# Short gated convolution on token rows, with neighbours' terms added by DMAs within SBUF

## The chip, the cores and the metric

The kernel runs on one core of a Trainium2 chip. The engines of the core are named as the profile names them: PE multiplies matrices (PEld is its loading of weights), DVE, ACT and POOL work element by element, SP only issues DMAs. The time is that of one execution on the device, in microseconds (us). Before the change it is 1527.46 us, the median of three executions that lie between 1526.65 and 1527.49.

## The reference

The program is an encoder of two layers over 512 tokens of width 2048. In each layer the normalised input `h` is multiplied by one wide matrix, and the product's columns are shared out: latents for an attention, a query for an attention over 256 memory tokens, a gate, and the three operands of a short convolution, 512 channels each. What bears on the change is this part:

```python
def short_gated_conv(gb, gc, xin, w):
    u = gc * xin
    up = jnp.pad(u, ((0, 0), (1, 1), (0, 0)))
    conv = up[:, :-2] * w[0] + up[:, 1:-1] * w[1] + up[:, 2:] * w[2]
    return gb * conv

z = h @ w_in[l]
q_lat, kv_lat, k_pe, gb, gc, xin, q_mem, gate = split_cols(z)
c_out = short_gated_conv(gb, gc, xin, conv_w[l])
y = jnp.concatenate([a_out, c_out, m_out], axis=-1) * jax.nn.silu(gate)
x = x + rmsnorm(y @ w_o[l], post_norm_g[l])
```

Each output token of the convolution takes the gated input `u` of the token before it, of itself and of the token behind it, each with a weight per channel. Everything is float32.

## The kernel before

**Products.** Each float32 operand is split into a high part and a rest (`hi`, `lo`), and one product becomes three matmuls on PE: lines 296, 297 (the one that takes the weights' low part, `wl`) and 298. A block of the weight matrix is multiplied by a scheme of seven products, P1 to P7, where sums of weight quarters and sums of input quarters (A11, A12, A22, S1 to S4) are multiplied. One such *group* yields two outputs of 512 columns for all four token tiles of 128 rows.

**Units.** The weights of a group pass as units of 256 rows by two times 512 columns (512 KB). SP loads a unit into one of eight buffers `wr`, six units ahead. Where a pass needs a sum of quarters, DVE adds another block (L200), or an accumulating DMA issued by POOL adds it in the buffer (L142), as soon as the buffer's earlier content has been read. ACT casts the unit to its high part `wh` (L212), DVE subtracts to get the low part `wl` (L216), and PE uses both for twelve matmuls. There are three buffers each for `wh` and `wl`.

**Order of passes.** The first two groups of a layer hold the convolution's operands: group 0 gives `gc` and `xi`, group 1 gives `gb` and its gate `gg`. Their passes run as P1, P2 of group 0; P1, P2 of group 1; P5, P6, P3 with P7, P4 of group 0; the same of group 1. After them comes group 2. At the end of a pass, DVE adds PE's result to the output tile (L500, L530, L533). When both operands of a token tile are there, `fin_u` (L698) multiplies `gc` by `xi`, and in the next group `fin_g` applies Silu to the gate on ACT (L705) and multiplies `gb` by it (L707).

**The convolution** (`conv_turn`, L837 to L846) stands between the steps of group 2, four times per layer, once for every 128 channels. PE turns four 128x128 blocks of `gc` (L823, into a bank `tps`) so that channels lie on the partitions and tokens along the row. There the neighbour is one element off, and a weight is one value per partition: DVE multiplies by the middle weight (L841), adds the two shifted terms (L842, L843), and multiplies by the turned `gb` (L846). The result `y` is the left operand of the output projection.

**What sets the order.** PE, SP and POOL work in the order in which the program writes their instructions. DVE and ACT are ordered by a scheduler through most of the program, but each works through its own list in order. Small operations can be put off: `pr.defer(cost, fn)` puts one in a queue, and it is written once the steps of the program have gathered as much room as its cost:

```python
spare = min(spare + room, 2.5)
while self.queue and spare >= self.queue[0][0]:
    cost, put_off = self.queue.pop(0)
    spare -= cost
    put_off()
```

`pr.until(there)` writes the queue out until a condition holds.

Of the kernel before, what the change touches and what calls it, by code (L numbers as in the profile page):

```python
# [251 lines left out]
def encoder(tc, x, mem, positions, pre_norm_g, w_in, q_norm_g, w_uq, kv_norm_g, w_ukv, conv_w,  # L252
# [35 lines left out]
    def scrap(name, w=512, dt=F32):  # L288
        return piece.tile([P, 512], dt, tag="piece", name=nm(name))[:, :w]
# [25 lines left out]
    def setup():  # L315
        ident = scrap("ident", P)
        make_identity(nc, ident)
        identr = const.tile([P, P], F32R, name="identr")
        nc.vector.tensor_copy(identr, ident)
        mhalf = const.tile([P, 4], F32, name="mhalf")  # L320
        nc.gpsimd.memset(mhalf, -0.5)
        G.update(ident=identr.bitcast(F32), identr=identr, mhalf=mhalf, junk=const.tile([P, 512], mybir.dt.bfloat16, name="junk"))
        rows = scrap("rows", P)[:KT * 2 * depth + 18 * depth]
        n = KT * depth
        nc.scalar.dma_start(rows[:n], pre_norm_g.rearrange("l (k p) -> (l k) p", p=P))
        nc.scalar.dma_start(rows[n:2 * n], mem_norm_g.rearrange("l (k p) -> (l k) p", p=P))
        m = 2 * n + 12 * depth
        nc.scalar.dma_start(rows[2 * n:m], conv_w.rearrange("l k (c p) -> (l k c) p", p=P))
        nc.sync.dma_start(rows[m:m + 4 * depth], q_norm_g.rearrange("l (k p) -> (l k) p", p=P))
        nc.sync.dma_start(rows[m + 4 * depth:], kv_norm_g.rearrange("l (k p) -> (l k) p", p=P))  # L330
        G["rows"] = rows

    def turn_constants():
        rows = G["rows"]
        n = KT * depth
        o = 2 * n + 12 * depth
        m = o + 6 * depth
        ps = bank("cps")
        nc.tensor.transpose(ps[:, :m], rows, G["ident"][:m, :m])
        cols = const.tile([P, m], F32, name="cols")  # L340
        nc.vector.tensor_copy(cols, ps[:, :m])
        for l in range(depth):
            G[f"g1_{l}"] = cols[:, l * KT:(l + 1) * KT]
            G[f"gm_{l}"] = cols[:, n + l * KT:n + (l + 1) * KT]
            G[f"cw{l}"] = cols[:, 2 * n + 12 * l:2 * n + 12 * (l + 1)].rearrange("p (k c) -> p k c", k=3)
            G[f"cq{l}"] = cols[:, o + 4 * l:o + 4 * (l + 1)]
            G[f"ckv{l}"] = cols[:, o + 4 * depth + 2 * l:o + 4 * depth + 2 * (l + 1)]

# [326 lines left out]
    def projection(l):  # L675
        def block(cols, w):
            def f(h, j, c):
                r = h * 1024 + c * 256
                return w_in[l, r:r + 256, cols[j]:cols[j] + w].rearrange("(a p) c -> p a c", p=P)
            return f  # L680

        C = {}

        def own(*names):
            def f():
                for n in names:
                    C[n] = slab(n).rearrange("p (t c) -> p t c", t=NT)
            return f

        def slot_of(a, b):  # L690
            return lambda i, j, tt: C[(a, b)[j]][:, 2 * i + tt, :]

        def fin_u(i, j, tt):
            t = 2 * i + tt
            key = "u", t
            C[key] = C.get(key, 0) + 1
            if C[key] == 2:
                nc.vector.tensor_tensor(C["gc"][:, t, :], C["gc"][:, t, :], C["xi"][:, t, :], op=ALU.mult)  # L698

        def fin_g(i, j, tt):  # L700
            t = 2 * i + tt
            key = "g", t
            C[key] = C.get(key, 0) + 1
            if j == 1:
                nc.scalar.activation(C["gg"][:, t, :], C["gg"][:, t, :], AF.Silu)  # L705
            if C[key] == 2:
                nc.vector.tensor_tensor(C["gb"][:, t, :], C["gb"][:, t, :], C["gg"][:, t, :], op=ALU.mult)  # L707

        def own_lat():
            two = [slab("lat") for _ in range(2)]  # L710
            C["lat"] = [two[t // 2][:, (t % 2) * 1024:(t % 2) * 1024 + 832] for t in range(NT)]

        lat = lambda i, j, tt: C["lat"][2 * i + tt][:, j * 416:(j + 1) * 416]
        skip = lambda i, j, tt: None
        L = G["left"]
        gs = [
            group(L, (l, 0), 512, block((O_GC, O_XI), 512), slot_of("gc", "xi"), HEAD if l else FIRST, fin_u,
                  by_two=l == 0),
            group(L, (l, 1), 512, block((O_GB, O_G + 1024), 512), slot_of("gb", "gg"), HEAD, fin_g),
            group(L, (l, 2), 512, block((O_G + 1536, O_QM), 512), slot_of("gm", "qm"), STEADY, skip),  # L720
            group(L, (l, 3), 416, block((0, 416), 416), lat, STEADY, skip),
            group(L, (l, 4), 512, block((O_G, O_G + 512), 512), slot_of("ga0", "ga1"), STEADY, skip),
        ]
# [95 lines left out]
    def turn4(view, j, dst=None):  # L819

        ps = bank("tps")
        for t in range(NT):
            nc.tensor.transpose(ps[:, t * P:(t + 1) * P], view(t)[:, j * P:(j + 1) * P], G["ident"])  # L823
        return ps
# [11 lines left out]

    def conv_turn(l, c, C):  # L837
        def f():
            u = turn4(lambda t: C["gc"][:, t, :], c)
            y, w = y_slab(2)[:, c, :], G[f"cw{l}"]  # L840
            nc.vector.tensor_scalar_mul(y, u, w[:, 1, c:c + 1])  # L841
            nc.vector.scalar_tensor_tensor(y[:, 1:], u[:, :S - 1], w[:, 0, c:c + 1], y[:, 1:], op0=ALU.mult, op1=ALU.add)  # L842
            nc.vector.scalar_tensor_tensor(y[:, :S - 1], u[:, 1:], w[:, 2, c:c + 1], y[:, :S - 1],  # L843
                                           op0=ALU.mult, op1=ALU.add)
            g = turn4(lambda t: C["gb"][:, t, :], c)
            nc.vector.tensor_tensor(y, y, g, op=ALU.mult)  # L846
# [483 lines left out]
    G["src"], G["dst"] = x[0], None  # L1330
    for l in range(depth):
        G["left"] = L = Left(True)
        C, gs, owns = projection(l)

        def use(L=L):
            G["left"] = L
# [41 lines left out]
        if l == 0:  # L1378
            put(a[:1])
            add(first.close)  # L1380
            add(turn_half(1, 1))
            add(lambda: left_half(0, (1,)))
            add(lambda: left_half(1, (1,)))
            add(lambda: first_rows(2))
            add(lambda: first_factor(3))
            add(lambda: first_rows(3))
            put(a[1:], b[:1])
            add(turn[2])
            add(lambda: right_half(0))
            put(b[1:3])  # L1390
            add(turn[3])
            add(lambda: right_half(1))
            put(b[3:])
        else:
            put(a, b)
        add(owns[1])
        put(a1, b1)
        put(*gs[0][2:], *gs[1][2:])
# [100 lines left out]
```

## Time and profile before

| | |
|---|---|
| median of three executions | 1527.46 us |
| the profiled execution | 1528.12 us |
| its span | 1525.9 us |
| mean granted clock of PE | 0.995 |
| bytes moved by DMAs | 270.61 MB, mean 177 GB/s |
| matmuls on PE | 7613 |

The span runs from the first to the last recorded instruction of that execution. In the rows below, "x8" is a number of instructions, "128x512" is partitions by elements, and a releaser behind "<-" is what ended the idle time before an instruction. In a timeline the columns are start in us, duration in us, engine, line and operation, output and inputs. A row that stands for several instructions gives the time from the first one's start to the last one's end. A PE instruction's duration contains its way through the pipeline, so matmuls overlap, and it is their starts that tell the pace. In the rows of DMAs the last number is the median time from issue to landing.

### The profile page before, as it was taken

What the parts mean: (1) busy time and instruction counts of PE and PEld (TensorE: products, weight loads), DVE (VectorE), ACT (ScalarE), POOL (GpSimd) and SP (SyncE); (2) the same over time, 40 slices, a digit from 0 to 9 for tenths busy, and PEclk for the clock granted to TensorE, in tenths of its full rate; (3) what the DMA queues carried; (4) which work ended last, traced back from release to release, by engine and by line L of the source; (5) the groups of instructions that cost most, each with busy time, mean ns of one, the idle gap of its engine ahead of it and who ended that gap; (6) DMA issues with size and microseconds to landing.
All of it is one profiled execution on the core that took longest, in us unless ns stands there. A gap on an engine that the chain in (4) does not pass through costs nothing.

```text
span 1525.9 us, 20317 instructions
## 1 busy us (share of the span) xinstructions
PE 1490.4 (98%) x7613; PEld 1277.0 (84%) x7613; DVE 1157.1 (76%) x1502; ACT 868.8 (57%) x1339; POOL 186.6 (12%) x197
## 2 busy tenths in 40 slices
PE   8999999999999999999999999999999999999995
PEld 7788888987898888888788888888988888888884
DVE  5987887575887668887798877886676776689777
ACT  8643534454667768645498443534454686775543
POOL 0212020221000000011230112010221000002111
PEclk9999999999999999999999999999999999999998
DMA  8989695979464111399696899685978421037873
GB/s 310 221 215 234 175 197 153 204 195 255 131 214 158 42 34 64 106 201 285 191 349 222 224 228 235 187 185 155 201 198 201 152 70 41 29 108 151 279 167 124
DMA packets 144206, 270.61 MB, mean 177 GB/s; under 512 B 17160, under 2 KB 39788, under 8 KB 140780
## 3 DMA queue, kind: packets, MB, share of 16 engines
q1 hardware_dynamic: 108904, 191.15, 39.1%
q0 software_dynamic: 35072, 78.13, 26.5%
q8 instruction: 59, 0.97, 0.3%
q14 instruction: 39, 0.32, 0.1%
q10 hardware_dynamic: 132, 0.05, 0.0%
HBM read 254.61 MB, written 14.68 MB: 176 GB/s over the span
## 4 chain that ended last, share of the span: by engine, by line
PE 85%; DVE 6%; ACT 4%; issue 2%; DMA 1%; POOL 1%; DVEq 0%; POOLq 0%; SPq 0%; ACTq 0%
PE P L297 20%; PE P L298 20%; PE P L296 20%; PE ptp L1063 2%; DVE wl L216 2%; ACT wh L212 2%; PE tps L823 2%; PE o L297 1%; PE sc L296 1%; PE sc L297 1%; PE sc L298 1%; PE o L298 1%; PE o L296 1%; PE sc L1043 1%; PE sc L1044 1%
## 5 line engine op out<-in xcount | busy, mean ns | idle before, releaser
L212 ACT CAST wh<-wr 128x1024 fp32r<-128x1024 f32 (+1 forms) x404 | 415.8, 1033 | 473.5 <-PE P L298 278.4
L216 DVE TENSOR_TENSOR wl<-wr,wh 128x1024 fp32r<-128x1024 f32 (+1 forms) x404 | 480.9, 1194 | 222.7 <-ACT wh L212 219.7
L296 PE MATMUL P<-wh,S 128*128 128x512 f32 (+1 forms) x896 | 346.7, 387 | 0.0
L297 PE MATMUL P<-wl,S 128*128 128x512 f32 (+1 forms) x896 | 345.1, 385 | 1.7 <-DVE wl L216 1.7
L298 PE MATMUL P<-wh,S 128*128 128x512 f32 (+1 forms) x896 | 344.3, 384 | 0.7 <-DVE S L434 0.7
L297 PE MATMUL P<-wl,A 128*128 128x512 f32 (+1 forms) x656 | 252.4, 385 | 6.3 <-DVE wl L216 6.3
L296 PE MATMUL P<-wh,A 128*128 128x512 f32 (+1 forms) x656 | 253.3, 386 | 0.9 <-ACT wh L212 0.9
L298 PE MATMUL P<-wh,A 128*128 128x512 f32 (+1 forms) x656 | 251.6, 384 | 0.5 <-DVE A L434 0.5
L297 PEld LDWEIGHTS P<-wl,S 128*128 128x128 f32 x896 | 168.7, 188 | 32.9 <-DVE wl L216 3.8
L298 PEld LDWEIGHTS P<-wh,S 128*128 128x128 f32 x896 | 168.5, 188 | 31.9 <-DVE S L434 1.1
L296 PEld LDWEIGHTS P<-wh,S 128*128 128x128 f32 x896 | 168.6, 188 | 29.7
L142 POOL DMA_DIRECT2D wr<-in_w_in_dram x84 | 101.6, 1210 | 554.1 <-DVE wl L216 400.4
L297 PEld LDWEIGHTS P<-wl,A 128*128 128x128 f32 x656 | 123.2, 188 | 29.7 <-DVE wl L216 8.4
L296 PEld LDWEIGHTS P<-wh,A 128*128 128x128 f32 x656 | 123.1, 188 | 23.8 <-ACT wh L212 2.1
L298 PEld LDWEIGHTS P<-wh,A 128*128 128x128 f32 x656 | 123.2, 188 | 23.4 <-DVE A L434 1.2
L200 DVE TENSOR_TENSOR wr<-wr,wr 128x1024 f32<-128x1024 f32 (+1 forms) x100 | 118.6, 1190 | 8.5 <-DMA wr<-in_w_in_dram 6.4
L1049 ACT ACTIVATE P<-sc,nm 128x512 f32<-128x512 f32 (+1 forms) x96 | 59.9, 625 | 36.7 <-DVE nm L1046 36.0
L1046 DVE TENSOR_REDUCE nm<-sc 128x1 f32<-128x512 f32 (+1 forms) x96 | 56.9, 595 | 12.3 <-PE sc L1044 6.8
L1052 ACT ACTIVATE P<-P,rec 128x512 f32<-128x512 f32 (+1 forms) x96 | 61.5, 658 | 5.9 <-DVE rec L1051 5.9
L142 POOL DMA_DIRECT2D wr<-in_w_o_dram x32 | 38.7, 1210 | 197.5 <-DVE wl L216 123.9
L302 DVE TENSOR_TENSOR PT<-ptp,PT 128x512 fp32r<-128x512 f32 (+1 forms) x96 | 56.1, 593 | 8.8 <-ACT PT L301 8.6
L226 ACT ACTIVATE wh<-wr,cols 128x512 fp32r<-128x512 f32 x64 | 43.9, 718 | 21.7 <-PE mk L297 7.7
(270 smaller groups left out, 2240.0 us busy)
## 6 DMA issues: line engine op xcount, KB each, us to landing
wr<-in_w_in_dram SPq DMA_DIRECT2D x172, 512.0 KB, 4.4
wr<-in_w_o_dram SPq DMA_DIRECT2D x72, 512.0 KB, 4.5
wr<-in_w_in_dram POOLq DMA_DIRECT2D x68, 512.0 KB, 7.2
wr<-in_w_in_dram SPq DMA_DIRECT2D x40, 416.0 KB, 3.8
wr<-in_w_o_dram POOLq DMA_DIRECT2D x32, 512.0 KB, 7.3
wr<-in_w_mk_dram SPq DMA_DIRECT2D x16, 512.0 KB, 5.3
wr<-in_w_mv_dram SPq DMA_DIRECT2D x16, 512.0 KB, 6.1
wr<-in_w_in_dram POOLq DMA_DIRECT2D x16, 416.0 KB, 5.9
```

The costliest lines, as they stand in the source:

```text
L142: engine.dma_start(dst, src, **kw)
L200: nc.vector.tensor_tensor(src, src, tiles[c], op=ALU.add)
L212: nc.scalar.copy(hi[:, :n], src)
L216: nc.vector.tensor_tensor(lo[:, :n], src, hi[:, :n].bitcast(F32), op=ALU.subtract)
L226: nc.scalar.activation(hi[:, h], src[:, h], AF.Copy, scale=g)
L296: nc.tensor.matmul(ps, ah, bh, start=first, stop=False, **kw)
L297: nc.tensor.matmul(ps, ah, bl, start=False, stop=False, **kw)
L298: nc.tensor.matmul(ps, al, bh, start=False, stop=last, **kw)
L302: nc.vector.tensor_tensor(lo, src, hi.bitcast(F32), op=ALU.subtract)
L1046: nc.vector.tensor_reduce(nmax, ps, axis=AX.X, op=ALU.max, negate=True)
L1049: nc.scalar.activation(pt, ps, AF.Exp, bias=nmax, accum_out=tot)
L1052: nc.scalar.activation(pt, pt, AF.Copy, scale=rec)
```

## The change

The convolution is computed with tokens on the partitions.

- The weights of the three taps come as rows, each sent to all 128 partitions by SP (`conv_rows`, 256 KB each). The columns of weights that the setup turned are gone.
- After L698 (now L696) three multiplies per token tile are put off with a cost of 0.7: `xi` becomes `u` times the middle weight, a new slab `zc` becomes `u` times the first, and `gc` becomes `u` times the last (L703).
- Behind the last of these twelve taps POOL issues four accumulating DMAs within SBUF. They add `zc` one partition down (L708) and `gc` one partition up (L709), 127 partitions of 2048 elements each, and then the rows that pass from one token tile to the next (L710, L711). L709 waits for L708 and L710 for L709, since they write the same slab.
- `fin_g` puts off one more multiply per token tile, `gb` by the finished `xi` (`weigh`, L728). The first of them waits for all four DMAs.
- `conv_turn` turns only `gb` (four transposes in place of eight), and ACT copies the bank to `y`.

```diff
@@ fin_u
             if C[key] == 2:
                 nc.vector.tensor_tensor(C["gc"][:, t, :], C["gc"][:, t, :], C["xi"][:, t, :], op=ALU.mult)
+                for k, name in ((1, "xi"), (0, "zc"), (2, "gc")):
+                    pr.defer(0.7, lambda k=k, name=name: taps(k, name, t))
+
+        def taps(k, name, t):
+            if name == "zc" and t == 0:
+                own("zc")()
+            nc.vector.tensor_tensor(C[name][:, t, :], C["gc"][:, t, :], C["w", k], op=ALU.mult)
+            if (k, t) != (2, NT - 1):
+                return
+            y, a, b = (C[n].rearrange("p t c -> p (t c)") for n in ("xi", "zc", "gc"))
+            n = (NT - 1) * 512
+            nc.gpsimd.dma_start(y[1:], a[:P - 1], accum_op=ALU.add)
+            nc.gpsimd.dma_start(y[:P - 1], b[1:], accum_op=ALU.add)
+            nc.gpsimd.dma_start(y[:1, 512:], a[P - 1:, :n], accum_op=ALU.add)
+            nc.gpsimd.dma_start(y[P - 1:, :n], b[:1, 512:], accum_op=ALU.add)
+
+        def conv_rows():
+            for k in range(3):
+                C["w", k] = scrap(f"cw{k}")
+                nc.sync.dma_start(C["w", k], conv_w[l, k].partition_broadcast(P))
@@ fin_g
                 nc.vector.tensor_tensor(C["gb"][:, t, :], C["gb"][:, t, :], C["gg"][:, t, :], op=ALU.mult)
+
+                def weigh():
+                    nc.vector.tensor_tensor(C["gb"][:, t, :], C["gb"][:, t, :], C["xi"][:, t, :], op=ALU.mult)
+                    C["conv"] = C.get("conv", 0) + 1
+                pr.defer(0.7, weigh)
@@ conv_turn
-            u = turn4(lambda t: C["gc"][:, t, :], c)
-            y, w = y_slab(2)[:, c, :], G[f"cw{l}"]
-            nc.vector.tensor_scalar_mul(y, u, w[:, 1, c:c + 1])
-            nc.vector.scalar_tensor_tensor(y[:, 1:], u[:, :S - 1], w[:, 0, c:c + 1], y[:, 1:], op0=ALU.mult, op1=ALU.add)
-            nc.vector.scalar_tensor_tensor(y[:, :S - 1], u[:, 1:], w[:, 2, c:c + 1], y[:, :S - 1],
-                                           op0=ALU.mult, op1=ALU.add)
-            g = turn4(lambda t: C["gb"][:, t, :], c)
-            nc.vector.tensor_tensor(y, y, g, op=ALU.mult)
+            pr.until(lambda: C.get("conv") == NT)
+            nc.scalar.copy(y_slab(2)[:, c, :], turn4(lambda t: C["gb"][:, t, :], c))
@@ main
             add(lambda: right_half(1))
+            add(conv_rows)
             put(b[3:])
         else:
-            put(a, b)
+            put(a)
+            add(conv_rows)
+            put(b)
```

The change moves lines (L696 in the new kernel is L698 before, L498 is L500, L531 is L533, L725 is L707) and the running numbers of tiles, but the number right behind `wl` and `wh` still counts the units. Three places in the lists of the engines matter below.

The first is DVE in layer 0 where group 1's P5 begins. `wl36` to `wl39` are the four units of that P5; L500 (L498) adds P4 of group 0, which shares the banks of its P6, and completes `gc` of the last two token tiles. Before:

```order
L216 TENSOR_TENSOR wl36_1074<-wr28_951,wh36_1073 128x1024
L200 TENSOR_TENSOR wr34_1016<-wr34_1016,wr35_1018 128x1024
L216 TENSOR_TENSOR wl37_1092<-wr30_971,wh37_1091 128x1024
L500 TENSOR_TENSOR gc_31_272<-gc_31_272,P6_70_798 128x512
L500 TENSOR_TENSOR gc_31_272<-gc_31_272,P6_71_799 128x512
L698 TENSOR_TENSOR gc_31_272<-gc_31_272,xi_32_273 128x512 x2
L216 TENSOR_TENSOR wl38_1116<-wr32_992,wh38_1115 128x1024
L216 TENSOR_TENSOR wl39_1138<-wr34_1016,wh39_1137 128x1024
```

With the change:

```order
L703 TENSOR_TENSOR zc_82_1022<-gc_31_271,cw0_57_519 128x512
L216 TENSOR_TENSOR wl36_1085<-wr28_956,wh36_1084 128x1024
L703 TENSOR_TENSOR gc_31_271<-gc_31_271,cw2_59_523 128x512
L200 TENSOR_TENSOR wr30_976<-wr30_976,wr31_978 128x1024
L498 TENSOR_TENSOR gc_31_271<-gc_31_271,P6_73_803 128x512
L498 TENSOR_TENSOR gc_31_271<-gc_31_271,P6_74_804 128x512
L216 TENSOR_TENSOR wl37_1104<-wr30_976,wh37_1103 128x1024
L696 TENSOR_TENSOR gc_31_271<-gc_31_271,xi_32_272 128x512 x2
L703 TENSOR_TENSOR xi_32_272<-gc_31_271,cw1_58_521 128x512
L200 TENSOR_TENSOR wr32_997<-wr32_997,wr33_999 128x1024
L200 TENSOR_TENSOR wr34_1025<-wr34_1025,wr35_1027 128x1024
L703 TENSOR_TENSOR zc_82_1022<-gc_31_271,cw0_57_519 128x512
```

The next row is `wl38`. Four more taps stand above this piece, two behind the first pair of L696, one behind `wl33` and one ahead of the first row, so that eight of the twelve taps stand between that pair and `wl38`; two sums (L200, of `wr32` and `wr34`) have moved from ahead of `wl37` to behind it. The other four taps stand between `wl40` and `wl43`.

The second place is DVE at the end of group 1 in layer 0, where the last pass (P4) takes its units from `wl52` on and L725 gates `gb`. Before:

```order
L216 TENSOR_TENSOR wl53_1407<-wr30_971,wh53_1406 128x1024
L707 TENSOR_TENSOR gb_57_540<-gb_57_540,gg_58_541 128x512 x2
L533 SCALAR_TENSOR_TENSOR gg_58_541<-P7_85_1296,gg_58_541 128x512
L500 TENSOR_TENSOR gb_57_540<-gb_57_540,P7_85_1296 128x512
L533 SCALAR_TENSOR_TENSOR gg_58_541<-P7_86_1297,gg_58_541 128x512
L500 TENSOR_TENSOR gb_57_540<-gb_57_540,P7_86_1297 128x512
L216 TENSOR_TENSOR wl54_1431<-wr32_992,wh54_1430 128x1024
```

With the change:

```order
L216 TENSOR_TENSOR wl53_1431<-wr30_976,wh53_1430 128x1024
L725 TENSOR_TENSOR gb_60_545<-gb_60_545,gg_61_546 128x512 x2
L728 TENSOR_TENSOR gb_60_545<-gb_60_545,xi_32_272 128x512 x2
L531 SCALAR_TENSOR_TENSOR gg_61_546<-P7_89_1318,gg_61_546 128x512
L498 TENSOR_TENSOR gb_60_545<-gb_60_545,P7_89_1318 128x512
L531 SCALAR_TENSOR_TENSOR gg_61_546<-P7_90_1319,gg_61_546 128x512
L498 TENSOR_TENSOR gb_60_545<-gb_60_545,P7_90_1319 128x512
L216 TENSOR_TENSOR wl54_1455<-wr32_997,wh54_1454 128x1024
```

Two of the new multiplies stand ahead of the four P7 rows and of `wl54`, and the first of them is the instruction that waits for the DMAs. In layer 1 the first pair of P7 rows stands ahead of L725, and the unit behind is `wl292`.

The third place is POOL in layer 0, with the change; the rows of L142 are the last two accumulates for P4 of group 1 and then the first for group 2:

```order
L142 DMA wr32_997<-in_w_in_dram 128x2x512
L142 DMA wr34_1025<-in_w_in_dram 128x2x512
L708 DMA xi_32_272<-zc_82_1022 127x2048
L709 DMA xi_32_272<-gc_31_271 127x2048
L710 DMA xi_32_272<-zc_82_1022 1x16x96
L711 DMA xi_32_272<-gc_31_271 1x16x96
L142 DMA wr44_1365<-in_w_in_dram 128x2x512
```

Before, the accumulate of `wr44` stands directly behind that of `wr34`; now four DMAs stand between them.

More of the change, by code (lines that the diff above doesn't have):

```diff
@@ L322, in setup @@
         G.update(ident=identr.bitcast(F32), identr=identr, mhalf=mhalf, junk=const.tile([P, 512], mybir.dt.bfloat16, name="junk"))
-        rows = scrap("rows", P)[:KT * 2 * depth + 18 * depth]
+        rows = scrap("rows", P)[:KT * 2 * depth + 6 * depth]
         n = KT * depth
@@ L326, in setup @@
         nc.scalar.dma_start(rows[n:2 * n], mem_norm_g.rearrange("l (k p) -> (l k) p", p=P))
-        m = 2 * n + 12 * depth
-        nc.scalar.dma_start(rows[2 * n:m], conv_w.rearrange("l k (c p) -> (l k c) p", p=P))
+        m = 2 * n
         nc.sync.dma_start(rows[m:m + 4 * depth], q_norm_g.rearrange("l (k p) -> (l k) p", p=P))
@@ L335, in turn_constants @@
         n = KT * depth
-        o = 2 * n + 12 * depth
+        o = 2 * n
         m = o + 6 * depth
@@ L344, in turn_constants @@
             G[f"gm_{l}"] = cols[:, n + l * KT:n + (l + 1) * KT]
-            G[f"cw{l}"] = cols[:, 2 * n + 12 * l:2 * n + 12 * (l + 1)].rearrange("p (k c) -> p k c", k=3)
             G[f"cq{l}"] = cols[:, o + 4 * l:o + 4 * (l + 1)]
@@ L724, in projection @@
         owns = [own("gc", "xi"), own("gb", "gg"), own("gm", "qm"), own_lat, own("ga0", "ga1")]
-        return C, gs, owns
+        return C, gs, owns, conv_rows
     def mem_load():
@@ L1332, in encoder @@
         G["left"] = L = Left(True)
-        C, gs, owns = projection(l)
+        C, gs, owns, conv_rows = projection(l)
         def use(L=L):
```

## The prediction, made before the changed kernel was run

> **What bounds the kernel now.** I read the busy shares first, then the chain of waits, then what PE waited for.
>
> ```profile
> span 1525.9 us, 20317 instructions
> PE 1490.4 (98%) x7613; PEld 1277.0 (84%) x7613; DVE 1157.1 (76%) x1502; ACT 868.8 (57%) x1339; POOL 186.6 (12%) x197
> PE 85%; DVE 6%; ACT 4%; issue 2%; DMA 1%; POOL 1%; DVEq 0%; POOLq 0%; SPq 0%; ACTq 0%
> PE P L297 <- DVE wl L216: 8.0, 10, 2.1
> ```
>
> PE is busy 98% of the span and carries 85% of the chain; its longest list of waits is 8.0 us in ten pieces, all for a low part `wl` that DVE makes. So the kernel is PE-bound, and the change can act in two ways only: it takes work from PE, or it makes PE wait where it does not wait now. DVE at 76% looks as if it had room, but that is a mean. I therefore read the stretches where the change puts DVE work, as busy times by engine (PE, weight loads, DVE, ACT, POOL), then granted clock, DMA share and GB/s:
>
> ```profile
> 109.91:127.39 17.48, 17.48 (x79) 14.46 (x78) 17.48 (x22) 7.00 (x7) 2.42 (x2) 1.00 0.87 271
> 127.39:137.50 10.11, 10.11 (x46) 8.40 (x45) 4.88 (x6) 3.54 (x4) 4.51 (x4) 1.00 1.11 199
> 908.53:926.02 17.49, 17.49 (x79) 14.49 (x78) 17.49 (x23) 6.80 (x7) 2.40 (x2) 1.00 0.85 266
> 194.00:214.00 20.00, 20.00 (x104) 16.84 (x103) 16.36 (x20) 7.70 (x9) 3.64 (x3) 1.00 0.84 184
> ```
>
> Where the gated input is finished and the taps will land (109.91 to 127.39 in layer 0, 908.53 to 926.02 in layer 1) DVE has no idle time at all, and PE none either. Just behind (127.39 to 137.50) DVE is busy 4.88 of 10.11 us. Where the convolution is done now (194 to 214) PE never waits, so DVE work removed there buys nothing.
>
> **What leaves PE.** Eight turns of four 128x128 transposes go (four of `gc` per layer). The stream of PE around one pair of turns:
>
> ```profile
> 194.25 0.39 PE L298 MATMUL P<-wh,A 128*128 128x512 f32 x1
> 194.48 0.60 PE L823 MATMUL tps<-identr,gc 128*128 128x128 f32 x4
> 194.91 0.60 PE L823 MATMUL tps<-identr,gb 128*128 128x128 f32 x4
> 195.27 0.48 PE L296 MATMUL P<-wh,S 128*128 128x512 f32 x1
> ```
>
> Products start 0.23 us apart (194.25 to 194.48), so eight transposes add 195.27 − 194.25 − 0.23 = 0.79, or 0.40 a turn. Eight turns: **−3.2 us**.
>
> **What leaves DVE and comes to ACT.** Per turn go L841, L842, L843 (of L842's form) and L846: 0.75 + 0.74 + 0.74 + 0.69 = 2.9 us of DVE. One ACT copy of the same form as L834 (597 ns) comes.
>
> ```profile
> L841 DVE TENSOR_SCALAR y<-tps,cols 128x512 f32<-128x512 f32 x8 | 6.0, 749 | 5.1 <-PE tps L823 5.1
> L842 DVE SCALAR_TENSOR_TENSOR y<-tps,cols,y 128x511 f32<-128x511 f32 x8 | 6.0, 744 | 0.0
> L846 DVE TENSOR_TENSOR y<-y,tps 128x512 f32<-128x512 f32 x8 | 5.5, 689 | 0.8
> L698 DVE TENSOR_TENSOR gc<-gc,xi 128x512 f32<-128x512 f32 x8 | 5.1, 680 | 0.0
> L834 ACT ACTIVATE y<-tps x24: 586/597/641, 376.0 to 1214.9; 128x512 f32<-128x512 f32 x24
> ```
>
> PE waits for none of the four, and ACT is busy 7.70 of 20 us there, so the copies hide: 0 and 0. Without that cover eight copies would cost 4.8 us.
>
> **Twelve taps per layer.** Each is a 128x512 multiply within SBUF like L698 (680 ns). Back to back such operations start 0.60 apart, as two do here, and the low part behind the second L698 pair ends at 127.39:
>
> ```profile
> 109.91 1.28 DVE L530 TENSOR_TENSOR xi<-P,xi 128x512 f32<-128x512 f32 x2
> 111.10 1.28 DVE L698 TENSOR_TENSOR gc<-gc,xi 128x512 f32<-128x512 f32 x2
> 122.64 1.22 DVE L216 TENSOR_TENSOR wl<-wr,wh 128x1024 fp32r<-128x1024 f32 x1
> 126.18 1.21 DVE L216 TENSOR_TENSOR wl<-wr,wh 128x1024 fp32r<-128x1024 f32 x1
> 132.45 1.23 DVE L216 TENSOR_TENSOR wl<-wr,wh 128x1024 fp32r<-128x1024 f32 x1 [3.42 <-ACT wh L212]
> 123.98 0.39 PE L297 MATMUL P<-wl,S 128*128 128x512 f32 x1
> 129.42 0.39 PE L297 MATMUL P<-wl,S 128*128 128x512 f32 x1
> 924.80 2.35 DVE L216 TENSOR_TENSOR wl<-wr,wh 128x1024 fp32r<-128x1024 f32 x2
> 926.97 0.39 PE L297 MATMUL P<-wl,S 128*128 128x512 f32 x1
> ```
>
> The order shows eight taps ahead of wl38, the third unit of P5 in the second group. PE first uses the first unit at 123.98; a unit is 12 products of 0.227, 2.72 us, so the third is due at 123.98 + 5.44 = 129.42. Since DVE has no gap before, eight taps (8 × 0.60 = 4.8) push its end from 127.39 to 132.2: PE waits **2.8 us**. The first two units stay in time by the same count: ahead of wl37 stand six taps and the two P6 evacuations more (3.6 + 1.2) but two sums L200 less (of wl37's size, 1.14 apart), so 2.5 more, from an end of 123.86 (the row at 122.64) to 126.4, with 126.70 as the due time. The last four taps (2.4) fall into gaps like the one of 3.42: 0. In layer 1 the order is the same at wl276, which ends at 926.02 (half of the pair at 924.80) and is due at 926.97: 4.8 − 0.95 = **3.85 us**. The price is not in doubt, since the form is L698's.
>
> **The weighting.** Two of the four new L728 stand ahead of wl54 (layer 0) and wl292 (layer 1), each 0.60.
>
> ```profile
> 167.82 1.29 DVE L707 TENSOR_TENSOR gb<-gb,gg 128x512 f32<-128x512 f32 x2 [0.72 <-ACT gg L705]
> 171.43 2.35 DVE L216 TENSOR_TENSOR wl<-wr,wh 128x1024 fp32r<-128x1024 f32 x2
> 172.94 0.39 PE L297 MATMUL P<-wl,A 128*128 128x512 f32 x1
> 968.28 2.35 DVE L216 TENSOR_TENSOR wl<-wr,wh 128x1024 fp32r<-128x1024 f32 x2
> 970.60 0.39 PE L297 MATMUL P<-wl,A 128*128 128x512 f32 x1
> ```
>
> wl54 ends at about 172.64 and is due at 172.94, a slack of 0.30; wl292 at 969.50, due 970.60, a slack of 1.10. Two L728 take 1.2: **0.9** and **0.1 us**.
>
> **The four accumulating DMAs.** The first L728 waits for all four, and behind it on DVE, which works in order, stand four P7 evacuations and wl54, so a late DMA goes to PE in full. Budget: POOL is free after its last P4 accumulate.
>
> ```profile
> 141.72 1.22 POOL L142 DMA_DIRECT2D wr<-in_w_in_dram  x1 [1.33 <-DVE wl L216]
> wr<-in_w_in_dram POOLq DMA_DIRECT2D x68, 512.0 KB, 7.2
> mTd<-mH POOLq DMA_DIRECT2D x2, 1024.0 KB, 5.3
> mH<-mTd POOLq DMA_DIRECT2D x2, 1024.0 KB, 9.6
> mL<-mTd POOLq DMA_DIRECT2D x2, 1024.0 KB, 12.7
> g<-in_post_norm_g_dram POOLq DMA_DIRECT2D x8, 256.0 KB, 6.4
> rows<-in_pre_norm_g_dram ACTq DMA_DIRECT2D x1, 16.0 KB, 1.7
> ```
>
> That is 142.9, plus PE's 2.8 and the four late taps' 2.4: 148.1. The first L728 is ready at 169.0 + 2.8 = 171.8, so 23.7 us are there. The chain is two transfers of 1016 KB one after the other, three further issues of 1.2 each (POOL's row) and a 6 KB landing. No row shows an accumulate within SBUF. Bounds: 2 × 5.3 + 3.6 + 1.7 = 15.9 and 2 × 12.7 + 3.6 + 6.4 = 35.4 (the landings of 16 KB and, far off, 256 KB), late by 0 or 11.7. I take 9.6 for each (512 KB accumulates take 7.2, and the first queues behind one) and 2.4 for the landing, near the 16 KB row: 19.2 + 3.6 + 2.4 = 25.2, **1.5 us late**, twice, since layer 1 has 0.5 us more at most between the same two points (926.97 to 965.88 against 129.42 to 167.82, where I take L707's start at 965.88).
>
> ```profile
> 965.88 1.29 DVE L707 TENSOR_TENSOR gb<-gb,gg 128x512 f32<-128x512 f32 x2
> ```
>
> [...]
>
> **Loads.** Three 256 KB broadcast loads per layer stand ahead of weight loads on SP. By the 6.4 of the broadcast `g` they hold the queue 19 us at worst, against six units of 2.72 that are loaded ahead, 16.3: 0 to 2.9 a layer, taken as 0, since transfers overlap. The 2 MB that the DMAs move share engines with weight loads that have units in hand too: 0.
>
> **Sum:** 2.8 + 3.85 + 0.9 + 0.1 + 3.0 − 3.2 = +7.45, on the profiled execution's 1528.12: 1535.6. That execution is 0.66 above the median of 1527.46, so **1535 us**.
>
> **The rivals.**
> (A, the forecast) Stalls at the third P5 unit and at the DMAs: with the DMAs late by 0 and 11.7 per layer, +4.5 to +27.9, or 1532 to 1555; its own likely range is 1531 to 1546, since the upper end needs the worst row for both transfers in both layers. Chance 0.74.
> (B) The stalls come, but a later PE waits less elsewhere. For it: 8.0 us of waits on `wl` exist, some of them after layer 0. Against: PE waits for nothing between 109.91 and 137.50, so nothing close by gives back. With the DMAs in time and half of the 8.0 recovered: +0.5, 1528. Chance 0.13.
> (C, the other side) The taps fit, the DMAs are in time, and only PE's relief remains: 1527.46 − 3.2 = 1524.3. Decided at 109.91 to 127.39: eight taps would have to take under 2.03 us, 0.25 each. Against: 17.48 of 17.48 busy. Chance 0.05.
> (D) The 127-row transfers are not spread over the DMA engines. Price by the software queue's row:
>
> ```profile
> q0 software_dynamic: 35072, 78.13, 26.5%
> ```
>
> 78.13 MB took 0.265 × 16 × 1525.9 = 6470 engine-us, 12.1 KB per us and engine. One engine alone would need 86 us for 1.04 MB, two in series 172; less the budget of 24, DVE stands about 148 us per layer, and PE with it: 1527.5 + 4.5 + 296 = 1828. [...] Against: all the queue's rows here have 128 partitions and show nothing of odd counts. Chance 0.08. [...]
>
> **How the numbers follow.** The time is A's, 1535. About 0.2% (3.05 us) can be told from no change, so slower means above 1530.5: nearly all of A with D and none of C, 0.80; B with A's lowest edge, 0.14; C, 0.06. The range leaves out C and D and holds A with most of B: 1529 to 1548.
>
> **What would show it.** Right: PE waiting on L297 for `wl` by 2 to 4 us near 130 and 928, and for one or two near 175 and 972; L728's idle time released by L709 to L711; no `tps<-gc`. If L728 shows no idle, the DMA term was too large (1532); if both transfers take 13 us, too small (1541 and more). Wrong at the root: no new wait of PE at the third P5 unit (then DVE's stretch was not the bound), or a gap of 100 us and more at L728 (D).

## The result: 1556 us, slower by more than was forecast

| | median, us | lowest to highest | executions |
|---|---|---|---|
| before | 1527.49 | 1526.65 to 1528.25 | 5 |
| with the change | 1556.13 | 1552.09 to 1558.71 | 5 |

The ratio is 1.0185, with a 95% interval of 1.0174 to 1.0196: 28.6 us slower. The forecast was 1535, 7.5 slower, with a range of 1529 to 1548. The direction was right, the size was not.

The page of the changed kernel, busy times first, then the chain that ended last; behind it the view of PE's waits (us in total, times, longest):

```profile
span 1554.9 us, 20277 instructions
PE 1498.1 (96%) x7581; PEld 1278.9 (82%) x7581; DVE 1154.5 (74%) x1502; ACT 873.3 (56%) x1347; POOL 192.8 (12%) x205
PE 67%; DVE 10%; DMA 9%; issue 8%; ACT 5%; POOL 1%; SPq 0%; DVEq 0%; POOLq 0%; ACTq 0%
```

```profile
PE P L297 <- DVE wl L216: 18.8, 19, 2.6
PE P L296 <- ACT wh L212: 10.9, 6, 5.3
```

PE's share of the chain fell from 85% to 67%, and DMAs went from 1% to 9%. The waits for `wl` rose from 8.0 to 18.8 us, as the prediction said they would. But there is a second list it had not expected: 10.9 us of waits for the high part `wh`, one of them 5.3 us long. And PE is busy 7.7 us longer although it has 32 instructions fewer, so some of its products ran slower.

The two traces hold the same products in the same order, so each can be set beside its twin. The growing difference of their start times splits the loss of the two profiled executions (in us):

| where (us in the changed kernel) | layer 0 | layer 1 |
|---|---|---|
| stalls at taps (119 to 134, 933 to 948) | 3.5 | 3.3 |
| stall at a unit loaded behind L708 (166, 979) | 6.8 | 4.6 |
| stall at `wl54` and `wl292`, behind L728 (189, 1000) | 2.8 | 1.7 |
| stall at the first turn of the convolution (215, 1024) | 1.8 | 0.9 |
| turns that are gone | −1.7 | −1.7 |
| products at a lower clock, and rest | 3.7 | 3.4 |
| sum | 16.9 | 12.2 |

The stall at the first turn is not one for the turn: PE waits there for a low part behind a sum (L200) that waited 5.74 us for a load. The largest row is the second. Its timeline on PE and ACT, and the windows behind it (busy time of PE, weight loads, DVE, ACT, POOL; then granted clock, DMA share, GB/s):

```profile
160.39 0.39 PE L298 MATMUL P<-wh,S 128*128 128x512 f32 x1
166.04 0.80 PE L296 MATMUL P<-wh,S 128*128 128x512 f32 x1 [5.26 <-ACT wh L212]
164.94 1.05 ACT L212 CAST wh<-wr 128x1024 fp32r<-128x1024 f32 x1 [9.91 <-DMA wr<-in_w_in_dram]
```

```profile
160.50:166.00 5.50, 0.28 (x2) 0.00 (x0) 0.00 (x0) 1.05 (x1) 0.84 (x1) 0.96 1.01 312
166.00:172.20 6.20, 5.70 (x13) 4.14 (x14) 4.92 (x5) 1.99 (x2) 0.00 (x0) 0.50 1.07 165
```

PE waits for a cast, and the cast waits for the load of its weights. No engine of the core was late; a transfer was. After the stall the clock granted to PE is 0.50 for some six us, and a product takes 0.43 us from start to start instead of 0.23.

The transfers of that stretch, by the view of DMA issues: first five weight loads of the kernel before, issued from 143 to 155 us, then those of the changed kernel issued from 147 to 158, with the DMAs of POOL beside them.

```profile
q1 hardware_dynamic: 1063, 2.05, 52.5%
q0 software_dynamic: 499, 0.95, 43.4%
wr<-in_w_in_dram SPq DMA_DIRECT2D x5, 512.0 KB, 4.4
```

```profile
q0 software_dynamic: 635, 1.81, 106.7%
q1 hardware_dynamic: 74, 0.15, 4.1%
wr<-in_w_in_dram SPq DMA_DIRECT2D x4, 512.0 KB, 14.5
xi<-zc POOLq DMA_DIRECT2D x1, 1016.0 KB, 16.4
wr<-in_w_in_dram POOLq DMA_DIRECT2D x1, 512.0 KB, 8.2
```

Loads of 512 KB whose median was 4.4 us take 14.5 when they are issued behind L708. And L708 itself takes 16.4, not 9.6. The rows of the two queues (packets, MB, share of the time of 16 engines) show why the loads are late: POOL's queue q0, with the packets of L708 and of the weight accumulates ahead of it, takes 106.7% of the time of the 16 engines, and q1, which carries SP's loads, moves 0.15 MB in 11 us where it moved 2.05 in 12. POOL and DVE in the changed kernel:

```profile
147.24 1.44 POOL L708 DMA_DIRECT2D xi<-zc  x1
163.94 0.84 POOL L709 DMA_DIRECT2D xi<-gc  x1 [15.26 <-DMA xi<-zc]
177.63 0.80 POOL L710 DMA_DIRECT2D xi<-zc  x1 [12.84 <-DMA xi<-gc]
184.01 1.29 DVE L728 TENSOR_TENSOR gb<-gb,xi 128x512 f32<-128x512 f32 x2 [1.70 <-DMA xi<-gc]
188.88 0.50 PE L297 MATMUL P<-wl,A 128*128 128x512 f32 x1 [2.60 <-DVE wl L216]
```

L708 is issued at 147.2, close to the 148.1 of the prediction. The chain then takes 36.6 us up to the last landing, not 25.2. L728 waits only 1.70 us in spite of that, because the stall at 166 had already moved DVE and PE back.

### The profile page after: what moved, and what is told of

It is laid out like the page before. It is cut to its first block, busy times and chain, and to the rows that moved or that the text cites. A ratio compares the mean times of both kernels' runs of the same rounds, so it can differ in the third digit from the quotient of the medians.

```text
span 1554.9 us, 20277 instructions
## 1 busy us (share of the span) xinstructions
PE 1498.1 (96%) x7581; PEld 1278.9 (82%) x7581; DVE 1154.5 (74%) x1502; ACT 873.3 (56%) x1347; POOL 192.8 (12%) x205
## 4 chain that ended last, share of the span: by engine, by line
PE 67%; DVE 10%; DMA 9%; issue 8%; ACT 5%; POOL 1%; SPq 0%; DVEq 0%; POOLq 0%; ACTq 0%
PE P L297 14%; PE P L298 14%; PE P L296 14%; DMA wr<-in_w_in_dram 4%; DVE wl L216 3%; DMA xi<-gc 2%; DMA xi<-zc 2%; ACT wh L212 2%; PE ptp L1080 2%; PE tps L846 1%; DVE wr L200 1%; PE o L297 1%; PE sc L296 1%; PE sc L297 1%; PE sc L298 1%
## 5 line engine op out<-in xcount | busy, mean ns | idle before, releaser
L216 DVE TENSOR_TENSOR wl<-wr,wh 128x1024 fp32r<-128x1024 f32 (+1 forms) x404 | 480.3, 1196 | 243.7 <-ACT wh L212 241.5
L296 PE MATMUL P<-wh,S 128*128 128x512 f32 (+1 forms) x896 | 349.8, 390 | 10.1 <-ACT wh L212 10.1
L297 PEld LDWEIGHTS P<-wl,S 128*128 128x128 f32 x896 | 170.2, 190 | 40.7 <-DVE wl L216 10.9
L142 POOL DMA_DIRECT2D wr<-in_w_in_dram x84 | 101.9, 1219 | 521.6 <-DVE wl L216 404.0
L200 DVE TENSOR_TENSOR wr<-wr,wr 128x1024 f32<-128x1024 f32 (+1 forms) x100 | 118.8, 1191 | 20.2 <-DMA wr<-in_w_in_dram 18.1
L1066 ACT ACTIVATE P<-sc,nm 128x512 f32<-128x512 f32 (+1 forms) x96 | 59.9, 625 | 36.6 <-DVE nm L1063 35.9
L142 POOL DMA_DIRECT2D wr<-in_w_o_dram x32 | 38.7, 1210 | 197.6 <-DVE wl L216 158.6
```

What stands on the lines that cost most here:

```text
L142: engine.dma_start(dst, src, **kw)
L200: nc.vector.tensor_tensor(src, src, tiles[c], op=ALU.add)
L216: nc.vector.tensor_tensor(lo[:, :n], src, hi[:, :n].bitcast(F32), op=ALU.subtract)
L296: nc.tensor.matmul(ps, ah, bh, start=first, stop=False, **kw)
L297: nc.tensor.matmul(ps, ah, bl, start=False, stop=False, **kw)
L1066: nc.scalar.activation(pt, ps, AF.Exp, bias=nmax, accum_out=tot)
```

## The experiments

Three theories were set against each other. Theory 1, contention: the accumulates hold the DMA engines, weight loads behind them are late, and PE stalls and then runs at a lower clock. Theory 2: taps and weighting displace the low parts on DVE. Theory 3: what costs is L728's wait for the chain of DMAs. The times below are medians; the kernel before had medians between 1526.8 and 1527.5 beside them.

**Without the DMAs.** The four `dma_start` calls of `taps` are taken out.

```diff
-            nc.gpsimd.dma_start(y[1:], a[:P - 1], accum_op=ALU.add)
-            nc.gpsimd.dma_start(y[:P - 1], b[1:], accum_op=ALU.add)
...
```

> The changed kernel without its four accumulating DMAs (the neighbours' terms are left out); taps, weighting and turns stay. Theory 1 (contention: the two 1016 KB transfers hold the DMA engines, weight loads issued behind them land 12 us late, PE stalls and then runs at a lower clock): all of that goes, what stays is the taps' displacement of DVE, some 3.9 in layer 0 and 3.5 in layer 1, about 1 for the weighting, less 3.5 for the turns, so 1531 to 1536. Theory 2 (DVE: the taps and the weighting displace the low parts, and the DMAs matter little): above 1548. Theory 3 (the first L728 waits for the chain of DMAs): 1531 to 1536 too; the next run separates it from theory 1.

Measured: 1537.62 us (four executions, 1532.1 to 1541.5). The DMAs cost 18.5 us of the 1556.1. What stays is above theories 1 and 3 and below theory 2: DVE's part is more than predicted as well.

**DMAs, but nobody waits for them.**

```diff
-                    nc.vector.tensor_tensor(C["gb"][:, t, :], C["gb"][:, t, :], C["xi"][:, t, :], op=ALU.mult)
+                    nc.vector.tensor_tensor(C["gb"][:, t, :], C["gb"][:, t, :], C["zc"][:, t, :], op=ALU.mult)
```

> The changed kernel with its DMAs, but L728 multiplies by zc, which the DMAs only read, so that nothing waits for them (the convolution's sum is left out of the result). Theory 1 (contention with weight loads): the stall and the half clock near 166 and 979 stay, the one near 189 and 1000 goes: 1546 to 1552. Theory 3 (the wait at L728 is what costs): 1531 to 1537. Theory 2 (DVE displaced): 1554 to 1558, since DVE does the same work.

Measured: 1548.54 us (1546.6 to 1550.3), as theory 1 said. The wait is worth 7.6 us, and 10.9 of the DMAs' 18.5 come without it. In this kernel's list of PE's waits the one for `wh` stands as in the changed kernel, 10.1 us against 10.9, with a longest of 4.0:

```profile
PE P L297 <- DVE wl L216: 14.5, 16, 2.1
PE P L296 <- ACT wh L212: 10.1, 6, 4.0
```

**The turns alone.** Taps, weighting, DMAs and the loads of the weight rows are out; `fin_g` counts the tile and nothing more.

```diff
-                for k, name in ((1, "xi"), (0, "zc"), (2, "gc")):
-                    pr.defer(0.7, lambda k=k, name=name: taps(k, name, t))
-                pr.defer(0.7, weigh)
+                C["conv"] = C.get("conv", 0) + 1
```

> The changed conv_turn alone: gb is turned, ACT copies, and there are no taps, no DMAs, no weighting and no loads of weight rows (the convolution is left out of the result). The turns' price of 0.43 each in the trace gives 1527.5 - 3.5 = 1524.0. If DVE's removed work at the turns is worth something to PE as well, below 1523; if the turns were hidden, 1527.

Measured: 1523.20 us, ratio 0.9970 (0.9959 to 0.9981), 4.0 us less than its kernel before (1527.2). So the turns' price holds, and the rest of the change costs 33 us: 14.4 for taps, weighting and the loads of the weight rows (1537.6 − 1523.2) and 18.5 for the DMAs.

**The transfers by themselves.** Five DMAs on two idle slabs in the attention of the kernel before, each waiting for the one ahead.

```diff
+        nc.gpsimd.dma_start(d[1:], z[:P - 1], accum_op=ALU.add)
+        nc.gpsimd.dma_start(d, z, accum_op=ALU.add)
+        nc.gpsimd.dma_start(d[1:], z[:P - 1])
+        nc.sync.dma_start(d[1:], z[:P - 1])
+        nc.gpsimd.dma_start(d[1:, :512], z[:P - 1, :512], accum_op=ALU.add)
```

> The kernel before, with five DMAs within SBUF added in layer 0's attention, where the DMA engines are nearly idle, each waiting for the one ahead: accumulates of 127 and of 128 rows of 2048, plain copies of 127 rows issued by POOL and by SP, an accumulate of 127 rows of 512. Theory 1 (contention stretched them to 16.3 and 13.3 us): the accumulate of 127 rows lands in 6 to 10 us here. Theory 4 (an accumulate within SBUF is slow by itself): 12 to 16 us here too, and the plain copies clearly less. 127 against 128 rows: alike if the rows are spread over the engines, several times longer if not.

The view of DMA issues, a row for each issue of POOL in order, with KB and us to landing; and, for the copy by SP, which has no landing there, its own issue and the one behind it in the timeline:

```profile
pd<-pz POOLq DMA_DIRECT2D x1, 1016.0 KB, 12.0
pd<-pz POOLq DMA_DIRECT2D x1, 1024.0 KB, 6.9
pd<-pz POOLq DMA_DIRECT2D x1, 1016.0 KB, 7.8
pd<-pz POOLq DMA_DIRECT2D x1, 254.0 KB, 5.7
```

```profile
572.93 0.73 SPq L1172 DMA_DIRECT2D pd<-pz  x1
617.36 0.86 POOL L1173 DMA_DIRECT2D pd<-pz  x1 [51.79 <-DMA pd<-pz]
```

Theory 4 holds in part: with the DMA engines nearly idle (a share of 0.13 from 540 to 580 us in the kernel before) the 127-row accumulate still takes 12.0 us, so of its 16.4 in the kernel most is its own. A surprise is that 128 rows in place take 6.9. A greater one is SP's copy of 127 rows: issued at 572.9, it held the next one until 617.4, some 44 us.

**Which shape is slow.** The same place, with other shapes.

```diff
+        nc.gpsimd.dma_start(d[:P - 1], z[:P - 1], accum_op=ALU.add)
         nc.gpsimd.dma_start(d[1:], z[:P - 1], accum_op=ALU.add)
+        nc.gpsimd.dma_start(d[:P - 1], z[1:], accum_op=ALU.add)
+        nc.gpsimd.dma_start(d[64:], z[:P - 64], accum_op=ALU.add)
         nc.gpsimd.dma_start(d, z, accum_op=ALU.add)
+        for k in range(4):
+            nc.gpsimd.dma_start(d[1:, k * 512:(k + 1) * 512], z[:P - 1, k * 512:(k + 1) * 512], accum_op=ALU.add)
```

> The kernel before with accumulating DMAs within SBUF in layer 0's attention, one behind the other: 127 rows in place, 127 rows one partition down, 127 one partition up, 64 rows 64 partitions down, 128 in place, and 127 rows one down in four pieces of 512 columns. The probe before had 12.0 us for 127 rows one down and 6.9 for 128 in place. If the count 127 makes it slow: in place is 12 too, and the 64 rows take about 4 to 7. If the shift by a partition makes it slow: in place takes 7, both shifts 12. If it was the first of the sequence: only the first takes 12.

In POOL's timeline each idle time before an issue is the time of the transfer ahead of it, less the issue:

```profile
545.21 0.94 POOL L1169 DMA_DIRECT2D pd<-pz  x1 [0.39 <-POOL pd L1168]
557.25 0.84 POOL L1170 DMA_DIRECT2D pd<-pz  x1 [11.11 <-DMA pd<-pz]
570.86 0.87 POOL L1171 DMA_DIRECT2D pd<-pz  x1 [12.77 <-DMA pd<-pz]
583.06 0.85 POOL L1172 DMA_DIRECT2D pd<-pz  x1 [11.34 <-DMA pd<-pz]
588.63 0.89 POOL L1173 DMA_DIRECT2D pd<-pz  x1 [4.72 <-DMA pd<-pz]
595.89 3.47 POOL L1175 DMA_DIRECT2D pd<-pz  x4 [6.37 <-DMA pd<-pz]
```

127 rows in place wait as long as shifted ones (11.1 against 12.8 and 11.3), so here it is the count and not the shift. 64 rows take 4.7, 128 rows 6.4. Each packet of 8 KB took 1.15 to 1.29 us with 127 rows and 0.63 to 0.67 with 64 or 128. Cut into four pieces of 512 columns the same 127 rows landed 9.9 us after the first issue.

**Plain copies in the same place.** In the quiet stretch their packets took about half as long (605 ns against 1149).

```diff
-            nc.gpsimd.dma_start(y[1:], a[:P - 1], accum_op=ALU.add)
-            nc.gpsimd.dma_start(y[:P - 1], b[1:], accum_op=ALU.add)
+            nc.gpsimd.dma_start(y[1:], a[:P - 1])
+            nc.gpsimd.dma_start(y[:P - 1], b[1:])
```

> The changed kernel with its two large DMAs as plain copies in the same place and order (they overwrite in place of adding, so the convolution's sum is wrong). In the probe the packets of a plain copy took 605 ns against 1149 ns of the shifted accumulate. Theory 1 (the time for which the packets hold the DMA engines ahead of the loads): the load behind the first lands in about 9 to 11 us in place of 16.4, the stall near 166 shrinks from 5.3 to 0 to 2 us, and the weighting waits for nothing: 1538 to 1546. Theory 3 (only the chain's length counts): 1538 to 1546 as well, but with the loads still 16 us. If neither: 1553 to 1558.

Measured: 1539.18 us (1536.4 to 1549.4), 17 less than the change. The loads issued behind the first copy landed after 11.5 us (the median of four) and the waits for `wh` shrink to 2.9 us from 10.9, about what they are without any DMAs (3.2):

```profile
PE P L297 <- DVE wl L216: 16.8, 19, 2.6
PE P L296 <- ACT wh L212: 2.9, 5, 0.9
```

With the packets' time nearly halved (143 us against 260 for both transfers) and their count, bytes and place kept, the stall at the loads in layer 0 shrinks to three waits of 0.24, 0.76 and 0.76 us, where it began with one of 5.26: theory 1. The first copy itself took 15.1 us from issue to landing, hardly less than the accumulate's 16.4, so it is not the length of the transfer that decides. One expectation failed: L728 still waited 1.72 us for the chain, and PE 2.62 behind it.

**Pieces in the same place.** Each whole accumulate becomes four of 512 columns.

```diff
-            nc.gpsimd.dma_start(y[1:], a[:P - 1], accum_op=ALU.add)
+            for i in range(0, NT * 512, 512):
+                nc.gpsimd.dma_start(y[1:, i:i + 512], a[:P - 1, i:i + 512], accum_op=ALU.add)
...
```

> The changed kernel with each 127x2048 accumulate cut into four of 127x512 columns, all issued in the same place. Alone in the attention four such pieces landed in 9.9 us where the whole took 13.3. Theory 1 by engine time (the pieces' packets hold the engines about 110 us in place of 145 to 155, over 16 engines): the load behind them lands in 10 to 12 us in place of 16.4 and the stall near 166 shrinks to 0 to 2: 1540 to 1550. If only being spread in time helps, and pieces in a row are as bad as the whole: 1553 to 1558.

Measured: 1546.04 us (1542.5 to 1548.1), 10 less than the change. The stall at the loads in layer 0 shrank as expected, from 5.26 us to waits of 0.80 and 0.76. But another grew: L728 (L730 in this kernel) waits 3.99 us for the chain instead of 1.70, and PE 4.89 behind it instead of 2.60.

```profile
180.36 1.29 DVE L730 TENSOR_TENSOR gb<-gb,xi 128x512 f32<-128x512 f32 x2 [3.99 <-DMA xi<-gc]
185.24 0.80 PE L297 MATMUL P<-wl,A 128*128 128x512 f32 x1 [4.89 <-DVE wl L216]
```

**Halves by rows.** 64 and 63 rows in place of 127.

```diff
-            nc.gpsimd.dma_start(y[1:], a[:P - 1], accum_op=ALU.add)
+            nc.gpsimd.dma_start(y[64:], a[63:P - 1], accum_op=ALU.add)
+            nc.gpsimd.dma_start(y[1:64], a[:63], accum_op=ALU.add)
...
```

> The changed kernel with each 127-row accumulate sent as 64 and 63 rows of 2048 (the same work and result). In the probe 127 rows had packets of 1150 to 1290 ns and 64 or 128 rows 630 to 674. Theory 1 by engine time: with short packets in both halves the two accumulates hold the engines as long as the plain copies did (1539.2), with one slow half some more: 1540 to 1549. If the time on the engines does not decide, or 63 rows are as slow as 127: 1552 to 1558.

Measured: 1548.76 us (1546.5 to 1554.1). The time lies in the expected interval, but not by the expected way: the packets' median stayed at 1.09 us, the load behind the two still took 15 us, and the stall at 165 stayed (3.9 us). In layer 0 the gain sits behind it: at `wl54`, where PE's stall is 1.0 instead of 2.6, and at the first turn, where none is left. That fewer rows make the packets short is therefore not shown for the kernel; only the quiet stretch shows it, with 1.15 to 1.29 us for 127 rows and 0.63 to 0.67 for 64 and 128.

**Everything late, no DMAs.** Taps written one behind each unit of P6 and of P3 with P7, weighting and turns in group 2's later steps.

```diff
-                for k, name in ((1, "xi"), (0, "zc"), (2, "gc")):
-                    pr.defer(0.7, lambda k=k, name=name: taps(k, name, t))
...
+        late = {k + 1: [f] for k, f in enumerate(C["tap"])}
+        for k, s in enumerate(gs[1][3] + gs[1][4] + gs[1][5]):
+            add(*s)
+            for f in late.pop(k + 1, ()):
+                add(f)
...
+        conv = [(f, []) for f in C["weigh"]] + [(conv_turn(l, c, C), []) for c in range(4)]
```

> The changed kernel without DMAs (neighbours' terms left out), with the twelve taps written one behind each unit of P6 and of P3 with P7 of group 1, so that none stands ahead of the third P5 unit, and the weighting and the turns written behind the first units of group 2's second pass. Theory 2a (the displacement at the third P5 unit and at wl54, with the lower clock behind those stalls, is the whole difference of 14.4 us between the kernel without DMAs, 1537.6, and the turns alone, 1523.2): 1523 to 1526. If taps and weighting cost DVE wherever they stand: 1530 or more.

Measured: 1523.78 us (1521.9 to 1525.5). The same 24 taps and eight weightings cost nothing here against the turns alone (1523.20), and neither do the loads of the weight rows, which this kernel has and that one has not: DVE's work is not what costs, its place is.

**Taps in the change's place, weighting late.** The turns stand late too, as in the run before.

```diff
+                for k, name in ((1, "xi"), (0, "zc"), (2, "gc")):
+                    pr.defer(0.7, lambda k=k, name=name: tap(k, name, t))
...
-        late = {k + 1: [f] for k, f in enumerate(C["tap"])}
+        late = {}
```

> No DMAs (neighbours' terms left out); the taps stand where the change has them, the weighting stands late. It lies between the kernel with both in the change's places (1537.6) and that with both late (1523.8). The prediction's terms say that the taps are most of it, 6.65 of 7.65 us: 1530 for the stalls as predicted, 1533 to 1536 if the stalls of some 4 us per layer and 1.5 us of lower clock behind each are the taps'. If the weighting were most of it: 1524 to 1528.

Measured: 1530.65 us (1528.8 to 1533.4). The taps' place costs 6.9 us (1530.65 − 1523.78); the prediction had 6.65. The weighting's place costs the other 7.0 (1537.62 − 1530.65), give or take some 3 us for the spread of the first; the prediction had 1.0.

**Late, in pieces.** Late taps as above, two 127x512 accumulates per token tile, the single rows and the weighting in group 2.

```diff
+        def down(t):
+            nc.gpsimd.dma_start(C["xi"][1:, t, :], C["zc"][:P - 1, t, :], accum_op=ALU.add)
+        def up(t):
+            nc.gpsimd.dma_start(C["xi"][:P - 1, t, :], C["gc"][1:, t, :], accum_op=ALU.add)
...
+            late.setdefault((5, 7, 9, 11)[t], []).append(d)
+            late.setdefault((6, 8, 10, 12)[t], []).append(u)
...
+        put(steps[:2])
+        add(C["edges"])
+        put(steps[2:4], weave(steps[4:], conv, 1), gs[2][4])
```

> The whole convolution with late taps as in the run beside it, and the DMAs cut into 127x512 pieces, two per token tile, issued from 146 us on between P6 and P3 with P7 of group 1, the rows between tiles and the weighting in group 2. Theory 1 (a 1016 KB accumulate holds every DMA engine for about 9 us ahead of the weight loads): pieces of a quarter delay each load by 2 to 4 us, which the loads' slack of about 3 us nearly covers, and nothing waits at the weighting: 1523 to 1530. If the volume and not the length counts: the same stall of 5 to 10 us per layer as in the change, 1535 to 1545.

Measured: 1523.47 us, ratio 0.9979 (0.9969 to 0.9990), with the whole convolution computed. It is faster than both kernels, by 3.3 us against its kernel before (1526.76), and no slower than the turns alone. Weight loads issued from 145 to 157 us land after 6.5 us, the pieces beside them after 5.3 and 8.5, and PE's waits are those of the kernel before:

```profile
wr<-in_w_in_dram SPq DMA_DIRECT2D x5, 512.0 KB, 6.5
xi<-gc POOLq DMA_DIRECT2D x1, 254.0 KB, 5.3
xi<-zc POOLq DMA_DIRECT2D x1, 254.0 KB, 8.5
```

```profile
PE P L297 <- DVE wl L216: 7.7, 9, 2.1
```

**Late, but whole.** The same kernel with the two accumulates of 127x2048.

```diff
-            nc.gpsimd.dma_start(C["xi"][1:, t, :], C["zc"][:P - 1, t, :], accum_op=ALU.add)
+            if t == NT - 1:
+                nc.gpsimd.dma_start(C["xi"][1:], C["zc"][:P - 1], accum_op=ALU.add)
...
```

> The version with late taps, late weighting and late turns (1523.5 with 127x512 pieces), but with the two whole accumulates of 127x2048 in place of the pieces, the first issued behind the last tap at about 148 us, as in the change. Theory 1 (a whole accumulate holds the DMA engines ahead of the weight loads): loads behind it land after 14 to 16 us, PE stalls 3 to 6 us per layer and runs at a lower clock behind it, 1531 to 1540. If the late taps and the late weighting were what the version gained by, and the pieces nothing: 1523 to 1527.

Measured: 1536.56 us (1535.7 to 1538.2), 13.1 more than in pieces. Loads issued from 146 to 156 us land after 11.6 us and the stall is back:

```profile
wr<-in_w_in_dram SPq DMA_DIRECT2D x4, 512.0 KB, 11.6
xi<-zc POOLq DMA_DIRECT2D x1, 1016.0 KB, 13.6
```

```profile
161.01 0.79 PE L296 MATMUL P<-wh,S 128*128 128x512 f32 x1 [3.78 <-ACT wh L212]
```

Here the weighting begins at 207.0, 31 us behind the multiply by the gate that it follows at once in the change, and no stall of PE follows its short waits for the single rows (2.19 us the first). The late taps cost PE no more than 0.5 us for a low part (at 149), so the stall at 161 is contention.

## Why the prediction was wrong, by its own steps

The runs give a ladder: 1527.2 before, −4.0 for the turns, +14.4 for taps and weighting in their places, +10.9 for the DMAs that nobody waits for, +7.6 for the wait: 1556.1. The run without DMAs is uncertain by some 3 us (its 95% interval is 1.0044 to 1.0084 of the kernel before), so the two steps beside it are too.

- **Turns, −3.2.** Right: −4.0 measured, and 0.43 a turn in the traces, where 0.40 had been read off the spacing.
- **DVE's and ACT's work at the turns, 0.** Right: with the turns alone no gain beyond the turns is clear (4.0 against 3.5 by the trace).
- **Taps, 2.8 + 3.85.** Right in place and sum: 6.9 in the difference of two runs, 3.5 and 3.3 in the trace. That the sum fits so closely is in part luck. At the third unit the stall is 2.5 us in layer 0 and 2.8 in layer 1, where 3.85 was forecast, and another 1.0 and 0.6 come at 120 and 934, in group 0's last pass, which the prediction did not have.
- **The broadcast loads of the weight rows, 0.** Right: they landed after 5.3 to 6.5 us, and the late version without DMAs, which has them, takes 1523.78 against 1523.20 of the turns alone.
- **Weighting, 0.9 + 0.1.** Mis-sized: 7.0 in the difference of two runs. The first pair costs what was said, 0.96 at `wl54` and 0.15 at `wl292` without DMAs. The second pair was not priced at all: it stands ahead of `wl58`, and in layer 0 of the run without DMAs a later sum L200 waits 6.33 us for a load, and PE 2.25 us for the `wl` behind it.

```profile
202.62 1.22 DVE L200 TENSOR_TENSOR wr<-wr,wr 128x1024 f32<-128x1024 f32 x1 [6.33 <-DMA wr<-in_w_in_dram]
203.76 3.49 DVE L216 TENSOR_TENSOR wl<-wr,wh 128x1024 fp32r<-128x1024 f32 x3
```

  Later low parts free their buffers later, so SP loads later. That is argued from the order of events; a run that moves the second pair alone was not made. It is also not the whole: in the run in which nobody waits for the DMAs the same pair stands in the same place, but the load took 5.1 us instead of 7.8, L200 waited 3.62, and PE did not stall. In layer 1 of the run without DMAs PE lost 0.2 us at that point. So the stalls of that trace make up some 3.7 of the 7.0. Part of the rest is lower clock, behind stalls that the taps cause too, since that differs from run to run (below).
- **DMAs' own time, 9.6 each.** Mis-sized: 16.4 and 13.4. The rows of 128 partitions were no guide to 127; alone in a quiet stretch such a transfer takes 12 to 13 us already.
- **Loads, 0.** This is the step that failed. It said that the 2 MB "share engines with weight loads that have units in hand too". They do not have them there. The load that came late was issued at 143.9 in the kernel before, landed at 150.4, and PE needed it at 156.4 with a cast of 1.05 between: some 5 us to spare, where the prediction counted on 16.3. In the changed kernel the same load was issued at 148.5, only 0.5 us later against PE's work, and landed at 164.8. Six units ahead is the limit of the program, but SP has to wait for a buffer: in the kernel before its waits between 130 and 170 us were 27.5 us for sums (L200) and 11.5 us for low parts (L216), which read the buffers that it fills next. And the engines had no room: the second window that the prediction quotes, which ends shortly ahead of the point where L708 is queued, had a DMA share of 1.11 at 199 GB/s, and from 143 to 155 us the two queues took 52.5% and 43.4%. The contention costs 10.9 us in the change and 13.1 in the late version, where it stands alone. By itself it would have left the time within the range (1535 + 10.9 = 1546); what the weighting (6.0) and the wait (4.6) cost beyond their forecasts brings it to 1556.
- **L728's wait, 3.0 in all.** Mis-sized: 7.6 in the difference of two runs. Set beside the run in which nobody waits, the trace has 1.8 and 1.6 us more at `wl54` and `wl292`, near the 1.5 for each layer that was forecast, and 1.8 and 0.9 more at the first turn, on the low part that is late in the run without DMAs too. The budget and the point were right, and so was the sign named for a term that is too small (both transfers over 13 us). That the stall at the point fits is luck: the chain was 11 us longer than estimated, and most of that was hidden by the stall the same DMAs made. Put into the prediction's own sum, the measured 36.6 us would have given 1558, close to the measured time, by a wait of 12.9 us per layer that the trace does not have.
- **The rival of one DMA engine** did not come: 127 rows by POOL were spread (147 us of packets in 12 us). For the copy issued by SP it did: 44 us, with 42 us of packets. What decides between the two was not shown.
- **No step had a lower clock.** It is worth 3 to 4 us a layer in the table above.

## What to carry to other kernels

A transfer is not free because nobody waits for it: here the DMAs cost 10.9 us without a wait, and loads issued behind the first of them landed after 14.5 us in place of 4.4. So look up the DMA share and the true slack of those loads (issue, landing, first use) at the moment of issue, not the depth of prefetch that the program allows. Cut it into pieces with gaps that the loads can use, as the late version did (1523.47 us against 1536.56 with whole transfers); pieces in a row won 10 us and made the wait at their end longer. And price added work on a full engine by where it stands: the same taps cost 6.9 us ahead of a due low part and nothing some units later.

## What was not expected of the hardware

- An accumulate within SBUF of 127 rows of 8 KB took 11.7 to 13.3 us in the quiet stretch, shifted or not; 128 rows took 6.9. The cause is open.
- A plain copy of 127 rows took 44 us issued by SP and 7.8 issued by POOL.
- Behind two stalls of the changed kernel PE ran at about half clock: granted 0.50 from 166.0 to 172.2, behind one of 5.26 us, and 0.57 from 189 to 193, behind one of 2.60. Shorter stalls were followed by a lower clock in one run and not in another. The same two stalls at the taps, 0.87 and 1.17 us in the run without DMAs and 0.89 and 1.16 in the run with taps in place and late weighting, were followed by a granted clock of 0.72 in one and 1.00 in the other:

```profile
134.00:140.00 6.00, 5.84 (x19) 4.72 (x20) 4.60 (x7) 1.58 (x2) 3.71 (x3) 0.72 1.05 268
```

```profile
132.90:138.90 6.00, 5.96 (x26) 4.92 (x27) 6.00 (x8) 1.47 (x2) 3.71 (x3) 1.00 1.07 268
```

  In the first 1.4 us are lost that the second does not lose. What decides whether the clock falls was not shown.
